# Sample-token outputs of a gated linear attention: states as the moving operand, results put in place by a 0/1 matmul

## The chip, the cores and the metric

The kernel runs on one core of one Trainium2 chip. The metric is device time in microseconds of one launch, as the median of several runs; a profiled execution of the same kernel has its own time and a trace. Lower is better.

## The reference, cut to what matters

The reference is one step of a two-layer decoder trunk with fp32 weights. The hidden width is 1024. It has 256 prompt tokens with 16 meta tokens ahead of them, and 8 running sequences of 8 new tokens each: 336 token columns in all, of which 64 are sample tokens. Each layer is a SwiGLU FFN, a mixer, and a second FFN.

The mixer projects the normed tokens to queries, keys, values, gates and a convolution input. One branch is a 31-tap depthwise convolution. The other is gated linear attention with 4 heads, keys of 128 and values of 256. Per sample sequence and head it computes

```
o_intra = (masked scores) v                  # 8 tokens among themselves
o_inter = q_t S0                             # (8 x 128) times the sequence's own state (128 x 256)
o       = o_intra + o_inter, then normed per head and scaled
S_new   = diag(decay) S0 + k^T v             # goes out as an output
```

The change concerns `o_inter` of the sample tokens: 8 sequences, 4 heads, 2 layers.

## The kernel before, in words

**Layout.** Activations are held with channels on the partitions and tokens on the free axis, in the order prompt (256), sample (64), meta (16). A projection of 1024 channels to 128 outputs is 8 steps of three matmuls (`mm3`: weights and activations are each split in a high and a low part), each with 336 moving columns, or 320 in the second layer. Weights stream in over SP's queue, are cast by ACT (`wh`, line 205) and the rest is subtracted on POOL or DVE (`wl`), three pieces ahead.

**Ticks.** In the mixer the large projections carry the small work along. After each `mm3` of `proj` the function `tick` pops one entry of the list `tasks` and then calls `fill`. In the stage of this study, the 15 gate projections (`gate_block`, 8 ticks each) carry four heads of attention. Nine ticks start head 0; then each head has 29 ticks. If ticks are counted from the first, task k of head h falls on tick 9 + 29h + k, and a gate block ends after ticks 7, 15, 23 and so on. At the end of a block DVE multiplies the bank by `rstd`, ACT applies the activation, and in eight of the blocks POOL multiplies the result into `wg`. Every engine works through its own queue strictly in the order in which the program emits.

**The filler.** The convolution runs on DVE as 248 taps a layer (31 taps for each of 8 channel blocks; a tap is one instruction over 272 prompt columns and one over 64 sample columns). Taps are emitted by `fill`, at most one a tick, by a cost account: `mm` books (n/2.4 + 2.5) ns, four times that for an fp32 operand, to `clock["pe"]`; each DVE instruction books 1.04 ns an element and 110 ns to `clock["dve"]`. A tap is emitted whenever

```
if filler[0] is not None and clock["dve"] + 7000.0 < clock["pe"]:
```

**A head's tasks.** `scores` and `prompt_state` come ahead of the head; `prompt_out` runs at tasks 0 and 3 and opens two PSUM banks `o`. `sample_out` adds `o_inter` into columns 256 to 319 of these banks, at tasks 7, 9, 11 and 13, four matmuls each: the state's 128x128 half is stationary and the 8 query columns of one sequence move. With task 13 comes `head_evict` (ACT copies both banks to the tile `ot`, line 675). `sample_state` at tasks 15 and 18 updates the states (matmuls `upds`, with a contraction of 32 rows at a time). The norm of the previous head comes at task 5 (`head_norm_a`: a matmul `nrm`, then ACT's square root `sd`) and task 10 (`head_norm_b`: DVE's reciprocal, two DVE multiplications into `ot`, two POOL multiplications of `wg` by `ot`, line 688). Tile `ot` has one buffer, so a new one waits until POOL's line 688 has read the old one:

```
st["ot"] = hp.tile([128, 2, T], F32, tag="ot", name="ot", bufs=1)
```

`kuT` holds the transposed keys; its fourth slot is a copy of the last token group with the lower 64 partitions zeroed, used by `prompt_state` part 0 for the meta tokens with all 128 rows.

Of the kernel before, what the change touches and what calls it, by code (L numbers as in the profile page):

```python
# [9 lines left out]
F32 = mybir.dt.float32  # L10
# [9 lines left out]
SEQ = 256  # L20
NS = 8
LS = 8
NSAMP = NS * LS
T = SEQ + NSAMP + META
TY = SEQ + NSAMP
# [4 lines left out]
HEADS = 4  # L30
DK = 128
DV = 256
# [25 lines left out]
C_CUM = C_SEQ + NS  # L58
TAIL = NSAMP + META
N_CUM = 2 * CHUNK + 2 * TAIL  # L60
NC_CONST = C_CUM + N_CUM

V_WIDTH = (352, 344, 344)
V_OFF = (0, 336, 680)
# [53 lines left out]
def trunk_kernel(ctx, tc, wts, x_in, vecs, consts, masks, wdecay, cache, state,  # L118
                 y_out, sp_out, ss_out, u_out):
    nc = tc.nc  # L120
    PE, ACT, POOL, SP = nc.tensor, nc.scalar, nc.gpsimd, nc.sync
# [7 lines left out]
    def mm(out, a, b, start, stop):  # L129
        n = 1  # L130
        for x in b.shape[1:]:
            n *= x
        clock["pe"] += (n / 2.4 + 2.5) * (4 if b.dtype == F32 else 1)
        PE.matmul(out, a, b, start=start, stop=stop)  # L134
# [6 lines left out]
    h = cst.tile([128, KB, T], F32, name="h")  # L141
# [3 lines left out]
    vec = cst.tile([128, NV], F32, name="vec")  # L145
    con = cst.tile([128, NC_CONST], F32, name="con")
    msk = cst.tile([128, 3 * 128], U32, name="msk")
# [6 lines left out]

    ident = con[:, C_ID:C_ID + 128]
    seqm = con[:, C_SEQ:C_SEQ + NS]

    def vcol(base, l, b, n=KB):
        return vec[:, base + l * n + b:base + l * n + b + 1]

    def bank(name, tag="mm", bufs=4):
        return psum.tile([128, 512], F32, tag=tag, name=name, bufs=bufs)
# [4 lines left out]
    def grp(g):  # L167
        return slice(g * 128, (g + 1) * 128)
# [174 lines left out]
    def mixer(l, norm, next_block):  # L343
# [6 lines left out]
        gp = gl.enter_context(tc.tile_pool(name="gla", bufs=1, reuse_waits="tile"))  # L350
# [2 lines left out]
        lal = mp.tile([128, 3, 512], F32R, tag="sb", name="lal")  # L353
        qt = gp.tile([128, HEADS, T], F32, name="qt")
        kt = gp.tile([128, HEADS, TP], F32, name="kt")
        kuT = gp.tile([128, 4, HEADS * DK], F32, name="kuT")
        v = gp.tile([128, 3, HEADS * DV], F32, name="v")
        dec = gp.tile([128, HEADS, 2 * NCH + NS], F32, name="dec")
        rT = gp.tile([128, 3], F32, name="rT")
# [6 lines left out]
        cum = kp.tile([128, N_CUM], F32R, name="cum")  # L366
# [5 lines left out]
        POOL.memset(lrs, 0.0)  # L372
        for c in (RANK, 64 + RANK):
            POOL.memset(lrs[:, :, c:c + 1], 1.0)
        ACT.copy(cum, con[:, C_CUM:])
        ACT.copy(wds[0:64], wdec[0:64])
        ACT.copy(wdr[64:128], wdec[64:128])
        POOL.tensor_tensor(out=wds[64:128], in0=wdec[64:128], in1=wdr[64:128].bitcast(F32), op=ALU.subtract)
        POOL.memset(kuT[0:64, 3], 0.0)
        cnorm = Norm()  # L380

        ready = [0]
# [149 lines left out]
        at = {0: decay_lr, 6: decay_alr, 14: decay_exp, 18: decay_ln, 70: decay_end}  # L532
# [20 lines left out]
        def transposes(hd):  # L553
            pt = bank("ptr", "aux", 2)
            for g in range(3):
                PE.transpose(pt[:, grp(g)], ku[:, hd, grp(g)], ident)
                clock["pe"] += 108.0
            hs = slice(hd * DK, (hd + 1) * DK)
            ACT.copy(kuT[:, 0:3, hs], pt[:, :384].rearrange("p (g d) -> p g d", g=3))
            ACT.copy(kuT[64:128, 3, hs], pt[64:128, grp(2)])  # L560

        for hd in range(HEADS):
            pk = bank("pk")
# [25 lines left out]
        hp = gl.enter_context(tc.tile_pool(name="heads", bufs=1, reuse_waits="tile"))  # L589
        s0 = {}  # L590

        def load_s0(i):
            if i < 2 * HEADS:
                t = hp.tile([128, NS // 2, DV], F32, tag="s0", name="s0", bufs=3)
                SP.dma_start(t, state[l, i // 2, i % 2])
                s0[i] = t

        for i in range(3):
            load_s0(i)

        def scores(hd, st):
            ps = bank("sc")
            for g in range(3):
                e = min((g + 1) * 128, n)
                mm(ps[:, g * 128:e], kt[:, hd, grp(g)], qt[:, hd, g * 128:e], True, True)
            DVE.copy_predicated(probs[hd % 2].rearrange("p g c -> p (g c)")[:, :n], msk[:, :n], ps[:, :n])

        def prompt_state(hd, st, part):
            ks = slice(hd * DK, (hd + 1) * DK)
            vs = slice(hd * DV, (hd + 1) * DV)  # L610
            pu = bank("upd", "aux", 2)
            if part == 0:
                sp = st["sp"] = hp.tile([128, 2 * NCH, DV], F32, tag="sp", name="sp", bufs=1)
                mm(pu[:, 0:DV], kuT[:, 3, ks], v[:, 2, vs], True, True)
                ACT.activation(sp[:, 0], pu[:, 0:DV], AF.Identity, scale=dec[:, hd, 1:2])
                return
            sp = st["sp"]
            for g in range(NCH):
                mm(pu[:, g * DV:(g + 1) * DV], kuT[:, g, ks], v[:, g, vs], True, True)
            for g in range(NCH):  # L620
                if g:
                    ACT.activation(sp[:, 2 * g], sp[:, 2 * g - 1], AF.Identity, scale=dec[:, hd, 2 * g + 1:2 * g + 2])
                DVE.scalar_tensor_tensor(out=sp[:, 2 * g + 1], in0=sp[:, 2 * g], scalar=dec[:, hd, 2 * g:2 * g + 1],
                                         in1=pu[:, g * DV:(g + 1) * DV], op0=ALU.mult, op1=ALU.add)
            SP.dma_start(sp_out[l, hd], sp[:, 2 * NCH - 1])
# [12 lines left out]
        def mask_ku(hd, st):  # L638
            km = st["km"] = hp.tile([64, NS, DK], F32, tag="km", name="km", bufs=1)
            src = kuT[0:64, 2, hd * DK:(hd + 1) * DK]  # L640
            POOL.tensor_tensor(out=km, in0=src.unsqueeze(1).to_broadcast([64, NS, DK]),
                               in1=seqm[0:64].unsqueeze(2).to_broadcast([64, NS, DK]), op=ALU.mult)

        def sample_out(hd, st, half, vb):
            t = s0[2 * hd + half]
            for i in range(NS // 2):
                s = half * (NS // 2) + i
                cs = slice(SEQ + s * LS, SEQ + (s + 1) * LS)
                mm(st["o", vb][:, cs], t[:, i, vb * 128:(vb + 1) * 128], qt[:, hd, cs], False, s == NS - 1)

        def sample_state(hd, st, p):
            km = st["km"]
# [18 lines left out]
        def head_evict(hd, st):  # L671
            ot = st["ot"] = hp.tile([128, 2, T], F32, tag="ot", name="ot", bufs=1)
            st["n"] = Norm()
            for vb in range(2):
                ACT.copy(ot[:, vb, 0:n], st["o", vb][:, 0:n])
                st["n"].add(ot[:, vb, 0:n], n)

        def head_norm_a(hd, st):
            st["sd"] = st["n"].mean_sqrt(ones_v, n)

        def head_norm_b(hd, st):
            r = st["n"].inverse(st["sd"], n)
            ot = st["ot"]
            for vb in range(2):
                b = 2 * hd + vb
                DVE.scalar_tensor_tensor(out=ot[:, vb, 0:n], in0=ot[:, vb, 0:n], scalar=vcol(V_GLA, l, b),
                                         in1=r[:, 0:n], op0=ALU.mult, op1=ALU.mult)
                POOL.tensor_tensor(out=wg[:, b, 0:n], in0=wg[:, b, 0:n], in1=ot[:, vb, 0:n], op=ALU.mult)

        hs = [{} for _ in range(HEADS)]  # L690

        def head_start(hd):
            st = hs[hd]
            return {0: lambda: (scores(hd, st), mask_ku(hd, st)), 1: lambda: prompt_state(hd, st, 0),
                    2: lambda: prompt_state(hd, st, 1)}

        def head_tasks(hd):
            st = hs[hd]
            at = {
                0: lambda: prompt_out(hd, st, 0),  # L700
                3: lambda: prompt_out(hd, st, 1),
                7: lambda: sample_out(hd, st, 0, 0),
                9: lambda: sample_out(hd, st, 0, 1),
                11: lambda: sample_out(hd, st, 1, 0),
                13: lambda: (sample_out(hd, st, 1, 1), head_evict(hd, st)),
                15: lambda: sample_state(hd, st, 0),
                18: lambda: sample_state(hd, st, 1),
            }
            if hd:
                at[5] = lambda: head_norm_a(hd - 1, hs[hd - 1])  # L710
                at[10] = lambda: head_norm_b(hd - 1, hs[hd - 1])
            if hd + 1 < HEADS:
                at.update({21 + k: f for k, f in head_start(hd + 1).items()})
            else:
                at[23] = lambda: head_norm_a(hd, st)
                at[28] = lambda: head_norm_b(hd, st)
            return [at.get(k) for k in range(29)]

        at = head_start(0)
        tasks.extend([at.get(k) for k in range(9)])  # L720
        for hd in range(HEADS):
            tasks.extend(head_tasks(hd))
# [78 lines left out]
        for b in range(2, KB):  # L801
            po = bank("po")
# [182 lines left out]
```

## Time and profile before

| what | value |
|---|---|
| median of 3 runs | 1649.36 us (1649.2 to 1652.94) |
| time of the profiled execution | 1653.15 us |
| its span, first to last instruction | 1651.4 us |
| TensorE (PE) busy | 98% of the span |
| VectorE (DVE) busy | 65% |
| ScalarE (ACT) busy | 44% |
| GpSimd (POOL) busy | 26% |
| mean granted TensorE clock | 0.991 |

Busy shares are means over the whole span. The two stages in which the heads run lie at about 398 to 505 us (first layer) and 1222 to 1322 us (second layer). An fp32 matmul shows as two matmul records, one for each pass; a line of the timeline that ends in x8 is four fp32 matmuls of the program.

### The profile page before, as it was taken

The page shows a single profiled execution, that of the slowest core. Times are in us where ns is not written, and L with a number is a line of the kernel's source. Part 1 is how long each engine was busy: PE and PEld are TensorE (multiplying, and loading weights), DVE is VectorE, ACT ScalarE, POOL GpSimd, SP SyncE. Part 2 cuts the span into 40 slices and gives each one's busy share as a digit, 9 for nine tenths or more (in the row PEclk, how much of TensorE's full clock was granted, in tenths as well). Part 3 has the DMA queues.
Part 4 walks back from the last instruction along what each step waited for, and adds up shares of the span by engine and source line. Part 5 has one row for each costly group of instructions (what it writes and reads, how often), then busy time and mean ns, then how long its engine had stood idle before and what let it go on. Part 6 is the DMA issues. An engine that isn't in the chain of part 4 may idle for free.

```text
span 1651.4 us, 27129 instructions
## 1 busy us (share of the span) xinstructions
PE 1615.1 (98%) x10612; PEld 1596.0 (97%) x10612; DVE 1080.0 (65%) x2159; ACT 727.6 (44%) x1154; POOL 424.7 (26%) x284
## 2 busy tenths in 40 slices
PE   8999999899999999999999999998999999999997
PEld 8999999899998999999999999998999989999997
DVE  7666446899986566564456654468998865666543
ACT  5433433743446344333343334347434464433432
POOL 0000016575575310000000000166756652000000
PEclk9999999999999999999999999999999999999999
DMA  5654445365453544444446444553644544445352
GB/s 200 203 181 126 133 152 163 112 182 166 131 173 115 154 140 153 141 130 141 152 142 212 141 134 131 157 150 112 192 156 142 173 136 151 148 153 153 116 171 78
DMA packets 76593, 247.56 MB, mean 150 GB/s; under 512 B 8625, under 2 KB 10929, under 8 KB 76209
## 3 DMA queue, kind: packets, MB, share of 16 engines
q1 hardware_dynamic: 75888, 240.34, 46.3%
q10 hardware_dynamic: 576, 5.49, 0.9%
q8 instruction: 83, 1.36, 0.3%
q14 instruction: 46, 0.37, 0.1%
HBM read 230.08 MB, written 15.71 MB: 149 GB/s over the span
## 4 chain that ended last, share of the span: by engine, by line
PE 85%; DVE 7%; ACT 4%; issue 2%; DMA 1%; POOL 0%; SPq 0%; DVEq 0%; POOLq 0%; ACTq 0%
PE pd L134 19%; PE pu L134 19%; PE pg L134 19%; PE pgate L134 6%; PE pw L134 4%; PE po L134 4%; DVE acc L112 2%; PE pa L134 2%; PE pga L134 2%; PE pv L134 2%; PE o L134 2%; PE pk L134 2%; PE pq L134 2%; DVE acs L112 1%; ACT wh L205 1%
## 5 line engine op out<-in xcount | busy, mean ns | idle before, releaser
L112 DVE TENSOR_TENSOR wl<-raw,wh 128x1024 fp32r<-128x1024 f32 (+1 forms) x320 | 349.3, 1108 | 228.1 <-ACT wh L205 227.6
L205 ACT CAST wh<-raw 128x1024 fp32r<-128x1024 f32 (+3 forms) x456 | 427.7, 956 | 74.4 <-issue 29.4
L207 POOL TENSOR_TENSOR wl<-raw,wh 128x1024 fp32r<-128x1024 f32 (+2 forms) x136 | 308.9, 2285 | 155.1 <-ACT wh L205 146.0
L270 POOL TENSOR_TENSOR ssum<-ssum,sq 128x336 f32<-128x336 f32 (+1 forms) x63 | 56.8, 901 | 1013.9 <-ACT sq L269 1013.8
L112 DVE SCALAR_TENSOR_TENSOR acc<-u,vec,acc 128x272 f32<-128x272 f32 (+1 forms) x480 | 235.2, 490 | 0.0
L134 PE MATMUL pg<-xh,wh 128*128 128x336 f32 (+1 forms) x704 | 222.8, 316 | 6.8 <-ACT wh L205 6.8
L134 PE MATMUL pg<-xh,wl 128*128 128x336 f32 (+1 forms) x704 | 221.8, 315 | 0.3 <-DVE wl L112 0.3
L134 PE MATMUL pu<-xh,wh 128*128 128x336 f32 (+1 forms) x704 | 221.6, 315 | 0.0
L134 PE MATMUL pu<-xh,wl 128*128 128x336 f32 (+1 forms) x704 | 221.6, 315 | 0.0
L134 PE MATMUL pd<-act_hi,wh 128*128 128x336 f32 (+1 forms) x704 | 221.0, 314 | 0.0
L134 PE MATMUL pu<-xl,wh 128*128 128x336 f32 (+1 forms) x704 | 220.9, 314 | 0.0
L134 PE MATMUL pg<-xl,wh 128*128 128x336 f32 (+1 forms) x704 | 220.9, 314 | 0.0
L134 PE MATMUL pd<-act_hi,wl 128*128 128x336 f32 (+1 forms) x704 | 220.3, 313 | 0.0
L134 PE MATMUL pd<-act_lo,wh 128*128 128x336 f32 (+1 forms) x704 | 220.2, 313 | 0.0
L134 PEld LDWEIGHTS pg<-xh,wh 128*128 128x128 f32 x704 | 132.7, 189 | 7.1 <-ACT wh L205 6.8
L112 DVE SCALAR_TENSOR_TENSOR acs<-u,vec,acs 128x64 f32<-128x64 f32 x480 | 135.5, 282 | 0.0
L326 ACT CAST act_hi<-pu 128x336 fp32r<-128x336 f32 (+1 forms) x88 | 38.5, 437 | 217.6 <-DVE pu L112 217.6
L134 PEld LDWEIGHTS pg<-xh,wl 128*128 128x128 f32 x704 | 132.6, 188 | 0.8 <-DVE wl L112 0.8
L134 PEld LDWEIGHTS pg<-xl,wh 128*128 128x128 f32 x704 | 132.7, 188 | 0.4
L134 PEld LDWEIGHTS pu<-xl,wh 128*128 128x128 f32 x704 | 132.6, 188 | 0.0
L134 PEld LDWEIGHTS pu<-xh,wl 128*128 128x128 f32 x704 | 132.6, 188 | 0.0
L134 PEld LDWEIGHTS pu<-xh,wh 128*128 128x128 f32 x704 | 132.6, 188 | 0.0
(200 smaller groups left out, 3277.4 us busy)
## 6 DMA issues: line engine op xcount, KB each, us to landing
raw<-in_wts SPq DMA_DIRECT2D x304, 512.0 KB, 3.6
raw<-in_wts SPq DMA_DIRECT2D x64, 384.0 KB, 3.6
raw<-in_wts SPq DMA_DIRECT2D x64, 320.0 KB, 3.0
s<-in_state SPq DMA_DIRECT2D x16, 512.0 KB, 4.5
out_ss<-s SPq DMA_DIRECT2D x16, 512.0 KB, 5.2
raw<-in_wts SPq DMA_DIRECT2D x16, 344.0 KB, 3.4
u<-in_cache ACTq DMA_DIRECT2D x2, 2424.0 KB, 11.0
out_u<-u SPq DMA_DIRECT2D x16, 303.0 KB, 4.6
```

The source lines that it names most:

```text
L112: return fn(*args, **kw)
L134: PE.matmul(out, a, b, start=start, stop=stop)
L205: ACT.copy(wh[:, :nk * nw], raw)
L207: eng.tensor_tensor(out=wl[:, :nk * nw], in0=raw, in1=wh[:, :nk * nw].bitcast(F32), op=ALU.subtract)
L270: eng.tensor_tensor(out=self.sum[:, 0:n], in0=self.sum[:, 0:n], in1=sq[:, 0:n], op=ALU.add)
L326: ACT.copy(ah[:, j, 0:n], pu[:, 0:n])
```

## The change

The four `sample_out` tasks of a head become one at task 9 with eight matmuls, each with the state of one sequence (128 x 256) as moving operand. The stationary operand is a 32-column slice of a tile `qz`, in which POOL (`spread_q`, with the head's start) has put the queries: sequence j of the first half at columns 32j to 32j+7, sequence j of the second half at columns 128+32j+8 to 128+32j+15, the rest zero. Result j lands on partitions 32j to 32j+31 of a PSUM bank `pso`; both halves add up there. ACT copies the bank to a tile `os`, which shares the one buffer of tag `ot`. At task 13 two matmuls (`sample_place`) multiply `os` by a constant 0/1 matrix of 64 columns and so add the result, transposed and in token order, into the banks `o`. The previous head's norm moves to tasks 2 and 5. `prompt_state` part 0 uses 32 rows of `kuT`'s third slot, and the fourth slot with its copy and memset goes.

```diff
-            ACT.copy(kuT[:, 0:3, hs], pt[:, :384].rearrange("p (g d) -> p g d", g=3))
-            ACT.copy(kuT[64:128, 3, hs], pt[64:128, grp(2)])
+            ACT.copy(kuT[:, :, hs], pt[:, :384].rearrange("p (g d) -> p g d", g=3))
...
+        qz = [hp.tile([128, 2 * (128 + LS)], F32, name=f"qz{i}") for i in range(2)]
+        for t in qz:
+            POOL.memset(t, 0.0)
...
-                mm(pu[:, 0:DV], kuT[:, 3, ks], v[:, 2, vs], True, True)
+                mm(pu[:, 0:DV], kuT[NSAMP:NSAMP + 32, 2, ks], v[NSAMP:NSAMP + 32, 2, vs], True, True)
...
-        def sample_out(hd, st, half, vb):
-            t = s0[2 * hd + half]
-            for i in range(NS // 2):
-                s = half * (NS // 2) + i
-                cs = slice(SEQ + s * LS, SEQ + (s + 1) * LS)
-                mm(st["o", vb][:, cs], t[:, i, vb * 128:(vb + 1) * 128], qt[:, hd, cs], False, s == NS - 1)
+        def spread_q(hd):
+            v4 = qz[hd % 2].rearrange("p (h x) -> p h x", h=2)[:, :, 0:128].rearrange("p h (j c) -> p h j c", c=32)
+            POOL.tensor_copy(out=v4[:, :, :, 0:LS],
+                             in_=qt[:, hd, SEQ:TY].rearrange("p (h j t) -> p h j t", h=2, t=LS))
+
+        def sample_out(hd, st):
+            po = bank("pso", "aux", 2)
+            for half in range(2):
+                for j in range(NS // 2):
+                    c = 32 * (half * (NS // 2) + j)
+                    mm(po[32 * j:32 * j + 32, 0:DV], qz[hd % 2][:, c:c + 32], s0[2 * hd + half][:, j],
+                       half == 0, half == 1)
+            os = st["os"] = hp.tile([128, 2, T], F32, tag="ot", name="os", bufs=1).rearrange("p a t -> p (a t)")
+            ACT.copy(os[:, 0:DV], po[:, 0:DV])
+
+        def sample_place(hd, st):
+            for vb in range(2):
+                mm(st["o", vb][:, SEQ:TY], st["os"][:, vb * 128:(vb + 1) * 128], place, False, True)
...
-            return {0: lambda: (scores(hd, st), mask_ku(hd, st)), 1: lambda: prompt_state(hd, st, 0),
+            return {0: lambda: (scores(hd, st), spread_q(hd), mask_ku(hd, st)), 1: lambda: prompt_state(hd, st, 0),
...
-                7: lambda: sample_out(hd, st, 0, 0),
-                9: lambda: sample_out(hd, st, 0, 1),
-                11: lambda: sample_out(hd, st, 1, 0),
-                13: lambda: (sample_out(hd, st, 1, 1), head_evict(hd, st)),
+                9: lambda: sample_out(hd, st),
+                13: lambda: (sample_place(hd, st), head_evict(hd, st)),
...
-                at[5] = lambda: head_norm_a(hd - 1, hs[hd - 1])
-                at[10] = lambda: head_norm_b(hd - 1, hs[hd - 1])
+                at[2] = lambda: head_norm_a(hd - 1, hs[hd - 1])
+                at[5] = lambda: head_norm_b(hd - 1, hs[hd - 1])
```

The constants grow by the 64 columns of the placing matrix.

## Rows read from the trace of the kernel before

**Rows 1.** Busy time by engine in the two stages of the heads.

```profile
core 0: us, PE busy (x) PEld busy (x) DVE busy (x) ACT busy (x) POOL busy (x), PEclk, DMA share, GB/s
...
398.00:505.00 107.00, 106.95 (x736) 100.47 (x736) 92.46 (x245) 49.74 (x84) 67.03 (x46) 1.00 0.48 154
...
1222.00:1322.00 100.00, 100.00 (x710) 94.33 (x709) 86.78 (x234) 45.49 (x77) 62.81 (x45) 1.00 0.50 164
```

**Rows 2.** Timeline of PE, head 0 of the first layer, one `sample_out` task.

```profile
413.70 0.32 PE L134 MATMUL pgate<-xh,wl 128*128 128x336 f32 x1
413.85 0.95 PE L134 MATMUL o<-qt,s 128*128 128x8 f32 x8
...
414.90 0.32 PE L134 MATMUL pgate<-xl,wh 128*128 128x336 f32 x1
```

**Rows 3.** Chain of waits, first layer: start, us, what; fp32 with 256 moving columns.

```profile
404.48 0.86 PE upd L134 x4
```

**Rows 4.** Timeline of PE, head 0, `sample_state`: the only matmuls on 32 rows.

```profile
420.96 0.32 PE L134 MATMUL pgate<-xh,wl 128*128 128x336 f32 x1
421.21 1.13 PE L134 MATMUL upds<-v,km 32*128 32x256 f32 x8
...
422.53 0.32 PE L134 MATMUL pgate<-xl,wh 128*128 128x336 f32 x1
```

**Rows 5.** Timeline of PE, head 1: the norm of head 0, the fourth `sample_out`.

```profile
436.79 0.73 PE L134 MATMUL nrm<-ssum,ones_v 128*128 128x336 f32 x2
...
443.72 0.95 PE L134 MATMUL o<-qt,s 128*128 128x8 f32 x8
```

**Rows 6.** Timeline of ACT, head 1; in brackets the idle time and its releaser.

```profile
437.51 0.45 ACT L575 ACTIVATE wg<-pgate 128x336 f32<-128x336 f32 x1 [5.17 <-DVE pgate L112]
...
440.21 0.54 ACT L285 ACTIVATE sd<-nrm,eps 128x336 f32<-128x336 f32 x1
...
449.05 0.44 ACT L675 COPY ot<-o 128x336 f32<-128x336 f32 x1 [4.94 <-POOL wg L688]
```

**Rows 7.** Timeline of DVE, head 1: a block's multiplication, taps, the reciprocal.

```profile
436.97 0.51 DVE L112 TENSOR_TENSOR pgate<-pgate,rstd 128x336 f32<-128x336 f32 x1
437.39 0.49 DVE L112 SCALAR_TENSOR_TENSOR acc<-u,vec,acc 128x272 f32<-128x272 f32 x1
...
437.99 0.50 DVE L112 SCALAR_TENSOR_TENSOR acc<-u,vec,acc 128x272 f32<-128x272 f32 x1
...
442.60 2.24 DVE L112 RECIPROCAL rstd<-sd 128x336 f32<-128x336 f32 x1
```

**Rows 8.** Timeline of POOL, heads 1 and 2: `wg` times the normed `ot`.

```profile
447.06 1.96 POOL L688 TENSOR_TENSOR wg<-wg,ot 128x336 f32<-128x336 f32 x2 [0.51 <-DVE ot L112]
...
469.75 1.96 POOL L688 TENSOR_TENSOR wg<-wg,ot 128x336 f32<-128x336 f32 x2 [2.49 <-DVE ot L112]
```

**Rows 9.** Waits of ACT's line 675 over the whole span: releaser, us, times.

```profile
  POOL wg L688: 19.1, 4
```

**Rows 10.** Waits of DVE from 410 to 440 us: us in total, times, longest.

```profile
DVE s L112 <- PE upds L134: 1.4, 2, 1.0
...
DVE pgate L112 <- PE pgate L134: 0.4, 1, 0.4
```

**Rows 11.** Timeline of DVE, head 2.

```profile
462.80 0.51 DVE L112 TENSOR_TENSOR pgate<-pgate,rstd 128x336 f32<-128x336 f32 x1
...
466.68 2.25 DVE L112 RECIPROCAL rstd<-sd 128x336 f32<-128x336 f32 x1 [0.37 <-ACT sd L285]
```

**Rows 12.** Timeline of PE, the fourth `sample_out` of heads 2 and 3.

```profile
468.68 0.95 PE L134 MATMUL o<-qt,s 128*128 128x8 f32 x8
...
493.11 0.95 PE L134 MATMUL o<-qt,s 128*128 128x8 f32 x8
```

**Rows 13.** Timeline of PE and of ACT, head 1 of the second layer.

```profile
1265.92 0.95 PE L134 MATMUL o<-qt,s 128*128 128x8 f32 x8
...
1270.63 0.43 ACT L675 COPY ot<-o 128x320 f32<-128x320 f32 x1 [4.87 <-POOL wg L688]
```

**Rows 14.** Busy time and granted clock where PE waits after the second layer's heads.

```profile
1346.00:1354.00 8.00, 5.52 (x20) 5.29 (x21) 5.62 (x9) 4.87 (x12) 3.21 (x2) 0.58 0.21 66
```

More of the change, by code (lines that the diff above doesn't have):

```diff
@@ L60 @@
 N_CUM = 2 * CHUNK + 2 * TAIL
-NC_CONST = C_CUM + N_CUM
+C_PLACE = C_CUM + N_CUM
+NC_CONST = C_PLACE + NSAMP
 V_WIDTH = (352, 344, 344)
@@ L156, in trunk_kernel @@
     seqm = con[:, C_SEQ:C_SEQ + NS]
+    place = con[:, C_PLACE:C_PLACE + NSAMP]
     def vcol(base, l, b, n=KB):
@@ L355, in mixer @@
         kt = gp.tile([128, HEADS, TP], F32, name="kt")
-        kuT = gp.tile([128, 4, HEADS * DK], F32, name="kuT")
+        kuT = gp.tile([128, 3, HEADS * DK], F32, name="kuT")
         v = gp.tile([128, 3, HEADS * DV], F32, name="v")
@@ L374, in mixer @@
             POOL.memset(lrs[:, :, c:c + 1], 1.0)
-        ACT.copy(cum, con[:, C_CUM:])
+        ACT.copy(cum, con[:, C_CUM:C_CUM + N_CUM])
         ACT.copy(wds[0:64], wdec[0:64])
@@ L378, in mixer @@
         POOL.tensor_tensor(out=wds[64:128], in0=wdec[64:128], in1=wdr[64:128].bitcast(F32), op=ALU.subtract)
-        POOL.memset(kuT[0:64, 3], 0.0)
         cnorm = Norm()
@@ L924 @@
     src_pos, dst_pos = pos[:, None], pos[None, :]
-    cumw = consts[:, C_CUM:]
+    cumw = consts[:, C_CUM:C_CUM + N_CUM]
     cumw[:, 0:CHUNK] = (np.where((src_pos >= HALF) & (src_pos <= dst_pos), 1, 0)
@@ L935 @@
         consts[s * LS:(s + 1) * LS, C_SEQ + s] = 1
+    for s in range(NS):
+        for t in range(LS):
+            half, j = divmod(s, NS // 2)
+            consts[32 * j + LS * half + t, C_PLACE + s * LS + t] = 1
     tri = np.triu(np.ones((CHUNK, CHUNK), np.uint32))
```

## The prediction

> **What bounds the kernel now.** I read the busy times by stage first. In both stages of the heads PE is busy without a gap, and DVE, the second busiest, works 92.46 of 107 us in the first layer and 86.78 of 100 us in the second [rows 1]. So work taken from PE there shortens the run, as long as nothing new makes PE wait; and DVE has under 15 us to spare in a stage. Then I read PE's timeline for the prices, and last the timelines of ACT, DVE and POOL around the norm of the previous head, because the change hangs a PE instruction on that chain.
>
> **PE: what goes and what comes.** A projection matmul starts every 0.15 us. One old `sample_out` task lies between two of them: 414.90 - 413.70 - 2 x 0.15 = 0.90 us [rows 2]. Four a head cost 3.60 us.
>
> The new task has 16 passes (8 fp32 matmuls, two passes each) with 256 moving columns. A pass of that width takes 0.86 / 4 = 0.215 us on the whole array [rows 3]. The trace has no matmul on a column tile; the nearest are the `upds` matmuls, 8 passes on two row tiles: 422.53 - 420.96 - 0.30 = 1.27 us [rows 4]. Eight passes one after another would take 1.72 us, four deep 0.86 us; so the two tiles ran side by side, and 0.41 us went to starting and switching. Sixteen passes on four column tiles are also four deep, so if they too run side by side they cost 1.27 us; one after another 16 x 0.215 + 0.41 = 3.85 us. I take 1.27, the row they are nearest to.
>
> `sample_place` is four passes with a full 128-column stationary operand and few columns, the form of the old task at 0.90 / 8 each: 0.45 us. `prompt_state` part 0 keeps its passes but now switches to a 32-row tile: nothing to 0.41 us, and I take 0.41. Sum for a head: 3.60 - 1.27 - 0.45 - 0.41 = 1.47 us less; eight heads, 11.8 us less, if PE never waits.
>
> The Trainium skill (TensorE: Matmul & The Clock Gate, Part 3, on packing small matmuls) says that a weight load slips past running matmuls only where the row groups differ, and the column tiles here share all their rows. No run here shows column tiles; by that rule they would go one after another, which is the third rival below.
>
> **The other engines.** ACT gains a copy of 256 columns a head, like the 0.44 us of [rows 6], and loses a small one; it has half the stage free [rows 1]. POOL gains `spread_q` and two memsets a layer and loses one memset; above, each costs no more than half of the 1.96 us that two line-688 instructions take [rows 8], below nothing. `spread_q` is wanted 18 ticks later and POOL idles 40 of 107 us [rows 1], so I cost it at nothing; without that cover it would be a microsecond a head. The larger constant load lies in the first FFN, at nothing. The second half's states are wanted two ticks earlier; I cost that at nothing too, since PE will be later, not earlier, in heads 1 to 3. `pso` is one more user of the two `aux` banks; it is free again before `upds` comes.
>
> **The new wait.** `sample_place` needs `os`; `os` needs the only buffer of `ot`; that is free when POOL's line 688 has read the previous head's `ot`. Before, this held back only ACT, 19.1 us in four waits [rows 9]. Now PE stands behind it, with the projections queued behind `sample_place`. In head 1, PE finished its fourth `sample_out` at 443.72 + 0.90 = 444.6 [rows 5] and ACT's copy could start only at 449.05 [rows 6], 4.5 us later. Moving the norm forward by 3 and 5 ticks has to buy that time and more.
>
> It does not, because the square root is held by something else. ACT works in order. The norm's new place, task 2, is the tick after a gate block's end; so `sd` is queued behind that block's activation, which waited 5.17 us for DVE, and started at 437.51 because DVE's multiplication ran at 436.97 [rows 6, 7]. `sd` ended at 440.21 + 0.54 = 440.75, though its matmul began at 436.79 [rows 5, 6]. An earlier matmul does not help.
>
> **DVE gets later.** The filler's account books the old `sample_out` at 16 x 4 x (8/2.4 + 2.5) = 373 ns a head; the new one with the placing at 8 x 4 x (256/2.4 + 2.5) + 2 x 4 x (64/2.4 + 2.5) = 3727 ns. A tap is booked at 570 ns. So each head sends out 5.9 taps earlier than before, within the limit of one a tick. Following the account tick by tick, 4 more taps are ahead of DVE at head 1's `head_norm_b` (tick 43) and 10 more at head 2's (tick 72); the taps run out at tick 82 in place of 98. A tap takes 0.60 us [rows 7]. In exchange DVE loses the waits for PE that it had, 1.4 + 0.4 = 1.8 us [rows 10].
>
> Head 1, first layer: DVE's multiplication and with it `sd` shift by 4 x 0.60 - 1.8 = 0.6 us, so the reciprocal starts at 441.4. DVE itself is there at 436.97 + 0.42 + 3 x 0.60 + 0.6 = 439.8 and waits 1.6 us. From the reciprocal's start to the end of line 688 it took 442.60 to 449.02, 6.4 us, in head 1 and 466.68 to 471.71, 5.0 us, in head 2 [rows 7, 8, 11]; I take 5.5. With the copy, `os` is there at 441.4 + 5.5 + 0.44 = 447.3. PE arrives at 443.72 - 1.47 (head 0) - 2.70 (three old tasks) + 1.27 + 0.41 = 441.2. It waits 6.1 us and is through at 447.8, where before it was at 444.6: 3.2 us late.
>
> Head 2: DVE passed the last multiplication ahead of this point at 462.80 + 0.42 = 463.2 [rows 11]. Now it is there at 463.2 + 10 x 0.60 - 1.8 + 1.6 = 469.0, and `sample_place` ends at 469.0 + 5.5 + 0.44 + 0.45 = 475.4; PE alone would be through at 447.8 + 25.0 - 1.5 = 471.3, so it waits 4.1 us. Before it was 468.68 + 0.90 = 469.6 [rows 12]: 5.8 us late.
>
> Head 3: the taps are gone and DVE is in step. PE gives 475.4 + 24.4 - 1.5 = 498.3 without a wait. From task 5 to task 13 PE needs 8 x 0.46 + 1.27 = 5.0 us, the chain 5.9, so 1.0 us more: 499.3 against 493.11 + 0.90 = 494.0 [rows 12], 5.3 us late.
>
> PE's clock: in the 8 us around the wait after the second layer's heads PE was idle 2.5 us and the mean granted clock was 0.58 of full speed, so most of the work ran at 1.2 GHz of 2.4; 20 matmuls took 5.52 us where 3.0 would do [rows 14], a loss of 2.5. The new waits are longer. A loss after head 1's wait falls into head 2's; one after head 2's counts, from nothing to 2.5 us, and I take 1.2. That makes 6.5 us a layer. In the second layer ACT's copy came 1270.63 - 1266.8 = 3.8 us after PE's last task, close to 4.5 [rows 13], so I take the same: 13 us in all.
>
> **The rivals.**
> 1. *The chain is in time* (faster). Then the 11.8 us come out: 1637.6 us. It decides at head 1: the reciprocal would have to start by 441.2 - 0.44 - 5.0 = 435.8. For it speaks that norm and place have moved apart by one tick; against it that `sd` ended at 440.75. Chance 0.15.
> 2. *The extra taps do not press* (no change). Head 1 still waits: 440.8 + 5.5 + 0.44 + 0.45 = 447.2, 2.6 late. Head 2's norm then starts at 463.2 and is ready before PE; head 3 loses about 1.0 against its 1.5 gain. Some 1 us a layer, up to 3 with the clock: 1650 to 1655. Against it: DVE's waits of rows 10 are all the slack it had. Chance 0.12.
> 3. *The column tiles run one after another*. A head then costs PE 3.85 in place of 1.27 us and gains nothing, but in heads 1 and 2 this only shortens the waits, whose end DVE sets. Head 3: 475.4 + 24.4 + 1.1 = 500.9, 6.9 late, and with a little for the clock 1664 to 1665. Chance 0.13.
> 4. *The same waits, dearer*: the chain at 6.4 us in both heads and the full 2.5 us of clock: some 10 us a layer, 1669 to 1675. Chance 0.12.
>
> **How the numbers follow.** My forecast, waits in heads 1 and 2 of each layer, has 0.48 and gives 1649.36 + 13 = 1662 us; the profiled execution, which was 1653.15 us and so 3.8 above the median, would come to 1666. Its own range is 1657 to 1669, from the chain at 5.0 or 6.4 us and the clock at nothing or 2.5. A difference of 0.3%, 5 us, is about what can be told from no change. Slower: 0.48 + 0.13 + 0.12 = 0.73; same 0.12; faster 0.15. The range of 1646 to 1673 leaves out the first rival and the end of the fourth.
>
> **What would show it.** Right: PE waits at the place matmuls for ACT's copy of `os`, which waits for POOL's line 688, about 6 and 4 us in heads 1 and 2 of each layer; the `sample_out` passes four deep within 1.3 us; the last block's taps some 16 ticks earlier; a lower granted clock after the waits. Wrong: no such wait or one under 2 us, which would mean that the norm got through ACT and POOL early; or DVE idle for PE in heads 1 and 2, which would mean that the taps do not press.

## The result, and the profile after

The changed kernel takes 1674.35 us (median of 4 runs, 1671.33 to 1677.47) against 1650.14 us for the kernel before in the same call (1649.2 to 1652.94): ratio 1.0145, 95% interval 1.013 to 1.0159. It is slower, by some 24 us where 13 were forecast, and 1.35 us past the end of the range. The profiled execution took 1673.21 us with a span of 1671.4, 20 us more than that of before.

Where it went is read in four steps. First the first layer's stage and, below it, the four stretches in the stages of the heads in which PE's granted clock is not full; this is the view of busy time by window, for the changed kernel:

```profile
core 0: us, PE busy (x) PEld busy (x) DVE busy (x) ACT busy (x) POOL busy (x), PEclk, DMA share, GB/s
399.00:516.00 117.00, 107.71 (x682) 93.69 (x681) 92.05 (x245) 49.81 (x86) 67.71 (x52) 0.91 0.45 142
...
445.00:456.00 11.00, 8.80 (x33) 7.12 (x35) 9.82 (x31) 5.61 (x12) 6.76 (x7) 0.53 0.19 57
476.00:487.00 11.00, 8.81 (x35) 7.00 (x35) 8.21 (x26) 3.39 (x7) 5.92 (x6) 0.53 0.41 138
1275.00:1289.00 14.00, 12.82 (x51) 10.51 (x51) 12.08 (x38) 6.82 (x13) 9.23 (x10) 0.52 0.13 38
1309.00:1316.00 7.00, 7.00 (x27) 5.51 (x28) 4.89 (x15) 3.24 (x8) 4.14 (x4) 0.51 0.16 44
```

In the stages of the heads PE had been busy all the time at full clock [rows 1]. Now it is idle for over 9 of the 117 us of the first layer's, the mean clock is 0.91, and there are four stretches almost wholly at the lower level, 1.2 GHz. They hold 27 to 51 matmuls in 7 to 14 us, under 4 in each microsecond, where PE did 6.9 before (736 in 107 us) [rows 1].

Second, PE's waits over the whole span (us in total, times, longest):

```profile
PE o L135 <- ACT os L661: 18.9, 6, 4.7
```

This is the wait that the prediction named, at the place matmuls for ACT's copy: 4.70 and 4.19 us in heads 1 and 2 of the first layer, 4.67 and 4.47 in the second, and two of at most 0.5 us in head 3. Nothing like it was there before. The four stretches of lower clock lie at the four long waits. Third, PE's timeline, with the prices in heads 0 and 1 and the places of heads 1 to 3:

```profile
404.14 0.32 PE L135 MATMUL pgate<-xh,wl 128*128 128x336 f32 x1
404.39 0.69 PE L135 MATMUL upd<-v,kuT 32*128 32x256 f32 x2
...
405.28 0.31 PE L135 MATMUL pgate<-xl,wh 128*128 128x336 f32 x1
...
415.89 0.32 PE L135 MATMUL pgate<-xh,wl 128*128 128x336 f32 x1
416.13 1.07 PE L135 MATMUL pso<-s,qz 128*32 128x256 f32 x16
...
417.39 0.32 PE L135 MATMUL pgate<-xl,wh 128*128 128x336 f32 x1
...
418.93 0.32 PE L135 MATMUL pgate<-xh,wl 128*128 128x336 f32 x1
419.09 0.55 PE L135 MATMUL o<-con,os 128*128 128x64 f32 x4
...
419.69 0.32 PE L135 MATMUL pgate<-xl,wh 128*128 128x336 f32 x1
...
442.19 0.32 PE L135 MATMUL pgate<-xh,wl 128*128 128x336 f32 x1
447.20 1.11 PE L135 MATMUL o<-con,os 128*128 128x64 f32 x4 [4.70 <-ACT os L661]
...
448.50 0.48 PE L135 MATMUL pgate<-xl,wh 128*128 128x336 f32 x1
448.78 0.48 PE L135 MATMUL pgate<-xh,wl 128*128 128x336 f32 x1
...
478.19 1.12 PE L135 MATMUL o<-con,os 128*128 128x64 f32 x4 [4.19 <-ACT os L661]
```

The prices are read as in [rows 2, 4]: from the projection matmul ahead to the second one behind, less two starts of 0.15. `sample_out`: 417.39 - 415.89 - 0.30 = 1.20 us. Place: 419.69 - 418.93 - 0.30 = 0.46. Part 0: 405.28 - 404.14 - 0.30 = 0.84. Behind the wait a projection takes 0.48 us where it took 0.32, and starts every 0.28 us in place of every 0.15: this is the lower clock seen matmul by matmul.

Fourth, what the copy waited for: ACT, DVE and POOL, in heads 1 and 2.

```profile
438.53 0.45 ACT L575 ACTIVATE wg<-pgate 128x336 f32<-128x336 f32 x1 [5.77 <-DVE pgate L113]
...
441.23 0.54 ACT L287 ACTIVATE sd<-nrm,eps 128x336 f32<-128x336 f32 x1
446.78 0.37 ACT L661 COPY os<-pso 128x256 f32<-128x256 f32 x1 [5.01 <-POOL wg L704]
...
441.81 2.25 DVE L113 RECIPROCAL rstd<-sd 128x336 f32<-128x336 f32 x1 [1.51 <-ACT sd L287]
...
444.74 2.01 POOL L704 TENSOR_TENSOR wg<-wg,ot 128x336 f32<-128x336 f32 x2 [2.37 <-DVE ot L113]
...
470.29 2.24 DVE L113 RECIPROCAL rstd<-sd 128x336 f32<-128x336 f32 x1
472.63 3.50 DVE L113 SCALAR_TENSOR_TENSOR ot<-ot,vec,rstd 128x336 f32<-128x336 f32 x2
...
473.22 2.55 POOL L209 TENSOR_TENSOR wl<-raw,wh 128x1024 fp32r<-128x1024 f32 x1
475.72 2.01 POOL L704 TENSOR_TENSOR wg<-wg,ot 128x336 f32<-128x336 f32 x2
...
477.76 0.37 ACT L661 COPY os<-pso 128x256 f32<-128x256 f32 x1 [4.62 <-POOL wg L704]
```

(Line 704 is line 688 of before.) Head 1 runs as foretold: gate block's activation, `sd`, reciprocal at 441.81, POOL, copy. In head 2 the chain from the reciprocal's start to POOL's end takes 477.73 - 470.29 = 7.4 us, not 5.5: line 704 stands behind POOL's split of a weight block in POOL's queue. The split ends at 475.77 and line 704 starts then. The two `ot` multiplications take 3.50 us where head 1's took 1.05, also beside the split, but they do not set the end: the first, by itself below, is done at 473.56, 2.2 us before line 704 starts, and the second at 476.13, before line 704's second half begins. In the second layer head 2's chain takes 1306.19 + 1.92 - 1300.54 = 7.6 us.

```profile
472.63 0.93 DVE L113 SCALAR_TENSOR_TENSOR ot<-ot,vec,rstd 128x336 f32<-128x336 f32 x1
...
1300.54 2.14 DVE L113 RECIPROCAL rstd<-sd 128x320 f32<-128x320 f32 x1
...
1306.19 1.92 POOL L704 TENSOR_TENSOR wg<-wg,ot 128x320 f32<-128x320 f32 x2
```

How late PE is, head by head, is seen from one mark: the time from the stage's first `sc` matmul to the first projection after the head's last sample operation, less the same time in the kernel before.

```
us later than before      head 0  head 1  head 2  head 3
predicted, a layer         -1.5    +3.2    +5.8    +5.3
changed kernel, layer 1    -1.5    +2.7    +8.7   +10.9
changed kernel, layer 2    -1.4    +2.8   +10.9   +12.9
```

Heads 0 and 1 are right within 0.5 us; the error comes in behind head 1.

### The profile page after: what moved, and what is told of

It reads as the page before. It is cut to its first block, busy times and chain, and to the rows that moved or that the text cites. A ratio compares the mean times of both kernels' runs of the same rounds, so it can differ in the third digit from the quotient of the medians.

```text
span 1671.4 us, 26957 instructions
## 1 busy us (share of the span) xinstructions
PE 1615.5 (97%) x10516; PEld 1580.5 (95%) x10516; DVE 1079.4 (65%) x2159; ACT 727.7 (44%) x1154; POOL 425.7 (25%) x294
## 4 chain that ended last, share of the span: by engine, by line
PE 79%; DVE 10%; ACT 5%; issue 3%; POOL 2%; DMA 1%; SPq 0%; DVEq 0%; POOLq 0%; ACTq 0%
PE pd L135 19%; PE pg L135 19%; PE pu L135 19%; PE pw L135 4%; PE po L135 3%; DVE acc L113 3%; PE pgate L135 3%; PE pa L135 2%; PE pga L135 2%; PE pv L135 2%; PE pk L135 2%; PE pq L135 2%; DVE acs L113 2%; ACT wh L207 1%; DVE rstd L113 1%
## 5 line engine op out<-in xcount | busy, mean ns | idle before, releaser
L135 PE MATMUL pgate<-xh,wh 128*128 128x336 f32 (+1 forms) x384 | 134.7, 351 | 0.0
```

## The experiments

All times are medians. The kernel before in the same call took 1650.07 us (own buffer, old booking, both at once, filling with 64 columns), 1651.19 (late norm, part 0, filling with 256 columns, early `sample_out`), 1650.53 (late norm with the new booking, early norm, later place) or 1650.93 (new booking alone). I had three theories: the shared buffer of `os` and `ot` alone; the taps that the filler now sends out early; and the lower clock behind each wait.

**Its own buffer for `os`** (the two `qz` made one for room):

```diff
-os = st["os"] = hp.tile([128, 2, T], F32, tag="ot", name="os", bufs=1).rearrange(...)
+os = st["os"] = hp.tile([128, DV], F32, tag="os", name="os", bufs=1)
```

> os gets a buffer of its own (the two buffers of qz become one to make room). Theory 1, all of the loss hangs on the shared buffer of os and ot: no wait is left, the clock stays up, and the lower PE price of 1.45 us a head shows: 1638 to 1642 us. Theory 2, the taps that the filler sends out earlier keep ACT's queue late too, since ACT's copy of os stands behind activations that wait for DVE: some 3 to 4 us of wait in head 2 of each layer and a spell of lower clock remain: 1650 to 1660 us.

Measured: 1671.18 us, ratio 1.0138 [1.0114, 1.0161]. PE's waits:

```profile
PE upds L135 <- DVE s L113: 12.7, 4, 3.8
...
PE pgate L135 <- ACT gate L578: 4.9, 2, 2.5
...
PE o L135 <- ACT os L660: 0.9, 2, 0.5
```

This is above what either theory gave. The wait at place is all but gone, and PE waits as long in other places (18.5 us in these three rows): 12.7 us for PSUM banks that DVE has not yet read, and 4.9 for one that ACT has not. So the shared buffer is not the whole cause: behind it stands, for the most part, DVE.

**The old booking**: the filler's account gets 373.3 ns a head for the new operations, as for the old `sample_out`, so the taps go out at the old pace; the buffer stays shared.

```diff
 po = bank("pso", "aux", 2)
+booked = clock["pe"]
...
+clock["pe"] = booked + 373.3
```

> The changed kernel, but the filler's account books the new sample_out and the placing as it booked the old tasks (373 ns a head), so that the taps go out when they did before. Theory 1, the shared buffer alone: the waits of 4.7 and 4.2 us stay, 1670 to 1676 us. Theory 2, the taps set head 2's wait and the square root's place in ACT's queue sets head 1's: one wait of 4 to 5 us in head 1 of each layer with its spell of lower clock, next to nothing in head 2: 1654 to 1662 us.

Measured: 1684.14 us, ratio 1.0205 [1.019, 1.0221]. Slower still, and above both theories. PE's waits, and then DVE and POOL in head 2:

```profile
PE o L135 <- ACT os L663: 20.5, 6, 4.1
```

```profile
467.14 2.25 DVE L113 RECIPROCAL rstd<-sd 128x336 f32<-128x336 f32 x1
...
470.08 2.56 POOL L209 TENSOR_TENSOR wl<-raw,wh 128x1024 fp32r<-128x1024 f32 x1
472.59 2.01 POOL L708 TENSOR_TENSOR wg<-wg,ot 128x336 f32<-128x336 f32 x2
```

Without the extra taps head 2 still waits (3.6 us), because the chain itself is 7.5 us long; and now head 3 waits too (3.4 us in the first layer, 3.5 in the second); that this comes from the taps left for it is argued, not shown. So with the shared buffer the waits do not need the taps.

**Both at once**: own buffer and old booking.

> Own buffer for os and the old booking together. Both theories: no wait at the placing matmuls, 1638 to 1642 us. If a loss of more than 5 us stays against that, something else in the change costs time (a wait for the states, a PSUM bank, the switches between tile forms).

Measured: 1662.35 us, ratio 1.0077 [1.0049, 1.0104]. Half of the loss is gone; both theories had no wait left. PE still waited 6.6 us for `os`, in head 3 of each layer. ACT there:

```profile
493.15 1.28 ACT L578 ACT_TABLE_LOAD   x1 [3.94 <-DVE pgate L113]
494.45 0.45 ACT L578 ACTIVATE gate<-pgate 128x336 f32<-128x336 f32 x1
...
495.73 0.38 ACT L662 COPY os<-pso 128x256 f32<-128x256 f32 x1
```

The copy needs nothing from the norm any more, but it is queued behind a gate activation, that one waits for DVE's multiplication, and DVE does the early norm first (reciprocal at 489.24, multiplication at 492.56).

**The late norm**: the same with the norm back at tasks 5 and 10. With the shared buffer this can't be had, since `os` at task 9 would need `ot` before the norm at 10 has read it.

```diff
-at[2] = lambda: head_norm_a(hd - 1, hs[hd - 1])
-at[5] = lambda: head_norm_b(hd - 1, hs[hd - 1])
+at[5] = lambda: head_norm_a(hd - 1, hs[hd - 1])
+at[10] = lambda: head_norm_b(hd - 1, hs[hd - 1])
```

> os in its own buffer, one qz, the filler booking what the old sample_out booked (as in the run that had both), and now the norm of the previous head back at its old tasks 5 and 10. Theory (in the run with both, head 3 waited because ACT's copy of os stood behind the gate block's activation, and that behind DVE's reciprocal and ot of the early norm): with the norm later the copy of os stands ahead of it in the queues, no wait of over 1 us is left at the place matmuls, no half-clock stretch but those of the kernel before, and the change's saving on PE shows in part: 1640 to 1650 us. Rival (DVE and ACT have no time to spare, wherever the norm stands): the waits come back at upds, pgate or place, and it stays at 1655 to 1665.

Measured: 1648.49 us (10 runs), ratio 0.9987 [0.9977, 0.9996]: just below both kernels. Its stage and its waits:

```profile
399.00:501.00 102.00, 99.48 (x672) 86.86 (x671) 89.74 (x243) 48.70 (x85) 67.11 (x51) 1.00 0.50 161
```

```profile
PE upds L135 <- DVE s L113: 2.6, 2, 1.4
PE o L135 <- ACT os L662: 2.5, 2, 1.4
```

The clock is full. By the mark above, head 3 is 2.6 us earlier than before in the first layer and 1.2 in the second; of the 4 x 1.47 = 5.9 us a layer that PE saves, some 2.5 go to the waits shown (5.1 us in two layers); the rest, 0.8 and 2.2 us, is not accounted for here. The theory was right on the time, and not quite on the waits: four are left, up to 1.4 us long.

**The late norm with the new booking**: own buffer, norm at 5 and 10, filler as in the change.

> os in its own buffer, one qz, norm of the previous head at tasks 5 and 10, but the filler booking the new operations at 3727 ns a head as the change does, so that the taps go out early. Theory (DVE's lag from early taps made the waits at upds and pgate in the run with its own buffer for os alone; the late norm does not cure it): waits of 2 to 4 us for DVE at upds come back, with half-clock stretches, 1655 to 1665 us. Rival (the early norm, forced by the shared buffer, was the whole of it; the booking does not matter once the norm is late): within 3 us of the run with the old booking, 1646 to 1652.

Measured: 1670.14 us, ratio 1.0128 [1.0112, 1.0143]. PE's waits, PE in head 1 and DVE there:

```profile
PE upds L135 <- DVE s L113: 18.6, 4, 7.5
```

```profile
446.22 0.32 PE L135 MATMUL pgate<-xh,wl 128*128 128x336 f32 x1
454.00 2.42 PE L135 MATMUL upds<-v,km 32*128 32x256 f32 x7 [7.46 <-DVE s L113]
...
453.07 1.65 DVE L113 SCALAR_TENSOR_TENSOR s<-s,dec,upds 128x256 f32<-128x256 f32 x4
```

One number in the filler's account is worth 21.7 us here. The waits, up to 7.5 us, were longer than the 2 to 4 expected, and the time lies above the 1655 to 1665.

**The new booking alone**, in the kernel before, without any new instruction:

```diff
+            if (half, vb) == (0, 1):
+                clock["pe"] += 3727.0 - 373.3
```

> The kernel before with one part of the change alone, and that one only in the filler's account: 3354 ns a head booked on top at task 9, so that a head books 3727 ns as in the changed kernel and 5.9 more taps go out in it. No instruction is added. Theory (the account alone makes DVE late for PE, as the run with own os, late norm and the new booking lost 21 us against the one with the old booking): waits of PE at upds in heads 1 and 2 of each layer and half-clock stretches behind them; PE has 1.5 us a head more to do here, so the waits are shorter than the 7.8 and 3.4 us there by about 1.5 a head: 1660 to 1668 us. Rival (only PE made shorter by the new sample_out runs into DVE; the old PE leaves DVE the time): within 3 us of before, 1648 to 1654.

Measured: 1670.26 us, ratio 1.013 [1.011, 1.015]; the theory's direction, dearer than its 1660 to 1668. PE's waits, and of DVE's in the first layer's stage the longest:

```profile
PE upds L134 <- DVE s L112: 11.7, 4, 5.6
...
DVE pgate L112 <- PE pgate L134: 8.1, 4, 6.0
```

DVE makes PE wait in heads 1 and 2 and then waits itself, once the taps are used up: the same work, badly spread.

**The other parts alone**, in the kernel before: part 0's 32-row tile, and the norm at tasks 2 and 5.

> The kernel before with one part of the change alone: prompt_state part 0 on the 32-row tile (its four-slot kuT stays, its fourth slot only unread). Theory (the price of switching the tile form is 0.42 us of PE a head and PE is the bound of the stage): 8 x 0.42 = 3.4 us slower, 1653 to 1654. Rival (PE's idle stretches in the stage take it up): 0 to 1 us.

> The kernel before with one part of the change alone: the previous head's norm at tasks 2 and 5 in place of 5 and 10. Theory (nothing on PE waits for the norm there, only ACT's eviction of ot does, and the square root does not come sooner, being held behind the gate block's activation): within 3 us of before, 1648 to 1654. Rival (the norm's place by itself makes DVE, ACT or POOL late for upds and the gate blocks): over 4 us slower, 1655 to 1665, and then part of the changed kernel's loss is not the place matmul's wait at all.

Measured: part 0 1652.79 us, ratio 1.0007 [0.9998, 1.0016], at most 2.6 us: this leaves out the 3.4 of its price on PE and takes in the rival's 0 to 1; norm 1651.29 us, ratio 1.0004 [0.9995, 1.0013], no change. The early norm is harmless until a PE instruction stands behind it.

**The clock.** Into the gap before place, in heads 1 and 2 of the changed kernel, 40 matmuls that add nothing: first of 64 columns with a moving operand of zeros, into `o`; then of 256 columns on ordinary data, into the unused half of `pso`'s bank, ahead of ACT's copy.

```diff
+for i in range(40 if hd in (1, 2) else 0):
+    PE.matmul(st["o", 1][:, SEQ:TY], xh[:, 0, 0:128], xh[:, 0:2, T:T + 32], start=False, stop=False)
```

```diff
+for i in range(40 if hd in (1, 2) else 0):
+    PE.matmul(po[:, 256:512], xh[:, 0, 0:128], xh[:, 0, 0:256], start=True, stop=True)
```

> The changed kernel with 40 matmuls of 64 zero columns ahead of the placing in heads 1 and 2, into the same bank; they add zero and fill PE's wait of 4.7 and 4.2 us with work. Theory C, the spells of lower clock after the waits cost some 4 us each: the clock stays at 2.4 GHz and the time falls by 8 to 16 us, to 1658 to 1666 us. Rival, the lower clock is hidden behind DVE's lag: 1671 to 1678 us, as without them.

> The changed kernel with 40 single-pass matmuls of 128x256 added behind sample_out in heads 1 and 2, into the unused half of its bank; nothing reads them. They give PE about 4.3 us of its ordinary kind of work where it otherwise stands idle before the place matmuls. Theory (the low clock after the waits costs about as much as the waits): the end of each wait is set by ACT's copy and does not move, but PE has no gap of more than 1.5 us there, the four half-clock stretches behind the places shrink or vanish, and the time falls by 10 to 17 us, to 1657 to 1664. Rival (the low clock costs little, since PE only works off what DVE lets it): the clock comes back and the time stays within 4 us of 1674. Second rival: the clock falls all the same, as with the 64-column matmuls: 1672 to 1680.

Measured with 64 columns of zeros: 1673.76 us, ratio 1.0139 [1.0115, 1.0163]. The gap is filled, the clock falls all the same:

```profile
447.00:460.00 13.00, 13.00 (x48) 10.64 (x49) 11.04 (x34) 6.46 (x13) 8.64 (x9) 0.50 0.14 40
```

```profile
442.02 4.55 PE L665 MATMUL o<-xh 128*128 128x64 f32 x40
446.87 1.05 PE L135 MATMUL o<-con,os 128*128 128x64 f32 x4 [0.30 <-ACT os L661]
```

Measured with 256 columns: 1667.31 us, ratio 1.0095 [1.0071, 1.0118]. The clock, in windows as above:

```profile
445.00:456.00 11.00, 10.65 (x67) 8.66 (x66) 11.00 (x34) 6.94 (x14) 7.34 (x8) 1.00 0.17 53
475.00:486.00 11.00, 11.00 (x69) 9.06 (x68) 10.78 (x33) 4.12 (x11) 5.19 (x6) 1.00 0.45 149
1274.00:1288.00 14.00, 12.36 (x57) 9.57 (x55) 12.53 (x39) 6.53 (x13) 9.62 (x9) 0.76 0.15 43
1307.00:1314.00 7.00, 7.00 (x48) 5.87 (x48) 6.77 (x20) 3.92 (x9) 5.05 (x5) 1.00 0.18 59
```

Three of four stretches are at full clock (the third has a new gap of 1.6 us of its own, at `upds`). PE's lateness in the first layer is then +2.3, +6.8, +6.2 us in heads 1 to 3, against +2.7, +8.7, +10.9: the clock cost 10.9 - 6.2 = 4.7 us there. In the second layer it is 12.9 - 10.2 = 2.7, with one stretch left. The gain of 7 us falls between the two stated bands: the clock costs much, but not as much as the waits. Of the 4.7 us, 8.7 - 6.8 = 1.9 stand at head 2's mark already: head 2's wait takes up a part of what head 1 loses, not all. The other 2.8 come behind head 2, and so do the 2.7 of the second layer. The two fillings differ in width, in data and in their place, so no run tells which of these kept the clock up.

**Placing moved**, on the late-norm version: `sample_out` at task 7, and place and eviction at task 14.

> As the run before it, with sample_out at task 7 in place of 9, so that ACT has six tasks (2.8 us) for the copy before the place. Theory: within 2 us of the run before it if no place waits there; faster by up to 5 us if one still does. Rival: the two aux banks are then held longer, and upd or upds waits for one: slower by 2 to 5 us.

> As the run with its own buffer for os, the old booking and the late norm, with place and eviction at task 14 in place of 13. In that run the place of head 3 waited 1.2 us in the first layer and about 1.4 in the second for ACT's copy, which stood behind a gate activation and a weight cast. Theory: one tick (0.46 us) of cover takes as much off each of the two waits and nothing else moves: 0 to 1 us faster than that run. Rival: the eviction a task later makes the next norm and upds later: 1 to 4 us slower.

Measured: 1650.83 us, ratio 1.0 [0.999, 1.0009], and 1649.5 us, ratio 0.9995 [0.9986, 1.0004]. Neither beats 1648.49. The early `sample_out` ends the waits for `os`, but those at `upds` grow from 2.6 to 3.5 us and the median is 2.3 us higher, as its rival had it. The later place cuts the waits for `os` from 2.5 to 1.6 us, as expected, with no gain in the time that could be told.

The parts side by side:

```
sample_out, place   os        filler's booking  norm at   us
none (before)       -         old               5, 10     1650
none                -         old               2, 5      1651.29
none                -         new               5, 10     1670.26
new (the change)    with ot   new               2, 5      1674.35
new                 with ot   old               2, 5      1684.14
new                 own       new               2, 5      1671.18
new                 own       old               2, 5      1662.35
new                 own       new               5, 10     1670.14
new                 own       old               5, 10     1648.49
```

Every version with the new booking lies between 1670 and 1675, whatever else it has. The early norm costs nothing by itself and 1662.35 - 1648.49 = 13.9 us once PE waits for `os` in the same queues. The two defects do not add; each is enough alone, so undoing one shows the other.

## Why the prediction was right, and where it was not

- **PE's prices: right.** `sample_out` 1.20 us (1.27 forecast), place 0.46 (0.45), part 0 +0.41 over the old 0.43 (+0.41). The column tiles run side by side: 16 passes in 1.07 us, where one after another would take 16 x 0.215 = 3.44, 3.2 times as long. The third rival is out. The Trainium skill's sentence that I weighed against it (TensorE: Matmul & The Clock Gate, Part 3, on weight loads and row groups) does not decide here; the same part's measured gain of 2.38 for three column tiles goes with this trace.
- **The saving of 11.8 us: there, but not to be had.** With most of the waits removed the version with the late norm got 1.2 to 2.6 us a layer of it at head 3, and its median is 2.7 us below that of the kernel before.
- **The wait, its chain and head 1: right.** Copy done at 447.15 (447.3 forecast), reciprocal at 441.81 (441.4). These agree better than they should, for the changed kernel entered the stage 0.9 us later; counted from its start the copy came 1.0 us earlier than forecast and PE 0.4 later, so PE waited 4.7 us and not 6.1. The first rival is out.
- **Head 2: right in kind, too short.** The reciprocal came at 470.29 (469.0); the chain took 7.4 us, and 7.6 in the second layer, not 5.5. In [rows 8] POOL was idle just ahead of line 688 both times, and the 6.4 us of head 1 already held one `ot` multiplication of 2.04 us beside a weight split; here line 704 stood behind such a split, which I did not look for.
- **The taps: the right cause, put in the wrong place.** I let them act only by making the norm late. With the shared buffer head 2 waits without them. But the booking by itself, in the kernel before, costs 1670.26 - 1650.93 = 19.3 us, through the PSUM banks of `upds` that DVE frees late. I worked out the 3727 ns and the 5.9 taps a head and never asked what they do without the wait. DVE was idle for PE as well, at `upds`, 1.2 us in head 1 and 3.1 in head 2, which I had named as a sign that the taps do not press; but that came behind PE's waits, when PE was late. The second rival is out.
- **The steps that failed: the clock, and head 2's end.** For the clock I took 1.2 us a layer from one stretch [rows 14], 2.5 at the most, and nothing for head 1, whose loss was to fall into head 2's wait. The two waits of a layer bring two stretches of 7 to 14 us. In the first layer 1.9 us of head 1's loss came through and 2.8 came behind head 2, 4.7 in all; in the second at least 2.7. I had sized it from an 8 us window, of which 2.5 us were idle. Head 2's end I put too early by the chain, 5.5 in place of 7.4 to 7.6 us, and in the second layer also by taking it "the same": counted from the stage's first `sc` matmul, head 2 is through at 75.9 us in the first layer and at 76.0 in the second, while the kernel before was through at 67.2 and 65.1. PE's own work is shorter there, the end that DVE and POOL set is not: 2.1 us that the forecast lacked.
- **Luck.** Without the clock the forecast would have nearly stood in the first layer, +6.2 against +5.3 at head 3. But two errors meet there: with PE's gaps filled head 2's reciprocal came 65.5 us into the stage, 1.2 earlier than the 66.7 forecast, and its chain took 2.0 longer.
- **The fourth rival came in.** "The same waits, dearer", 1669 to 1675 us, had a chance of 0.12, and my range left out its end, where the time fell. Its terms were still too small: 6.4 us for the chain and 2.5 for the clock.
- **The sum.** By the mark, 5.3 + 1.2 = 6.5 us a layer became 10.9 and 12.9: 10.8 us more. Of these the clock is 4.7 - 1.2 = 3.5 in the first layer and at least 2.7 - 1.2 = 1.5 in the second; the rest, 0.9 and 4.9, is head 2's later end. Of the 4.9, 2.1 are the second layer taken as the first; the other 2.8 hold the chain and a clock stretch that I could not part from it. Some 4 us of the 23.8 come back outside the heads; 3 of them lie between the layers, where the granted clock of the kernel before had a stretch at half (1128.9 to 1135.7 us) that the changed kernel lacks; of the fourteen profiled kernels eight have one there. So the profiled executions differ by 20.0 us. The medians differ by 24.2, because before's profiled execution was 3.0 us above its median and this one 1.1 below.

What stays open: why the second `ot` multiplication takes 2.65 us in head 2 where one by itself takes 0.56. In both kernels every one that takes over 0.6 us runs beside POOL's split of a weight block. The taps do not lengthen there: in the changed kernel 98 of 272 columns ran wholly inside such a split and took 0.50 us, as outside. A tap adds into PSUM and reads one tensor from SBUF, `ot`'s multiplications read two. No run took the split away, so that this is the reason, and that moving the split would shorten the chain, is not shown.

## What to carry to other kernels

When a change makes one engine's instruction cheaper or dearer, look at what plans by it: a filler that books 3.7 us for 1.7 us of work hands DVE its work too early, and that alone cost 19.3 us where the whole change cost 24.2. The old account was no truer, 0.37 us for 3.60 of work; what counts is when the work goes out. When a new instruction of the bounding engine depends on a buffer, follow not only the buffer but every queue that its producer stands in; taking away one wait here only showed the next. The gaps of 4.2 to 4.7 us on PE cost their own length and then a stretch at half clock, of which the part counts that no later wait takes up.

## What the runs showed of the hardware

Four column tiles, each with 32 stationary columns and all 128 rows, run side by side in fp32: 16 passes of 256 columns in 1.07 us. Each wait of 4.2 to 4.7 us on PE brought 7 to 14 us at 1.2 GHz. The Trainium skill (TensorE: Matmul & The Clock Gate, on the oscillation of the clock gate) counts half of the throttled time as lost; by that, an estimate for the 37.4 busy microseconds of the four stretches is 19 us. Ending three of the four gave back 7, since part of the loss in one head falls into the next head's wait; that rule gives a loss of PE's time, not of the whole. And a PE that the profile shows busy all through the gap, with 40 matmuls of 64 columns on zeros, came out of it at half clock all the same (0.50), where 40 of 256 columns on ordinary data came out at full clock (1.00).
